# First value projection of a hybrid decoder on one core: tokens turned raw, the norm's root applied behind the matmuls, two column groups interleaved, the tiles normalized in place beside the last group

## The chip, the core and the metric

The kernel runs on one core of a Trainium2 chip. The core has a matrix engine (PE), a vector engine (DVE), an activation engine (ACT), GpSimd (POOL) and a queue engine (SP); DMAs are issued from SP, ACT and POOL. Each engine takes its instructions in a fixed order; what orders them between engines are semaphores. The metric is the device time of the program in microseconds (us), the median of its runs. Of a run one execution is profiled, and all rows below are of such an execution.

## What is computed

One step of a two-layer decoder: 1024 prompt tokens, 16 meta tokens and 8 x 8 sample tokens, 1104 rows of width 1024 in all. The change is in the first layer's input, of which these lines matter:

```python
def rmsnorm(x, g):
    r = lax.rsqrt(jnp.mean(xf * xf, axis=-1, keepdims=True) + EPS)
    return xf * r * g
...
p = xn @ w_in                       # xn = rmsnorm(h, norm_a): 1024 -> 3088 columns
q = heads(p[..., :HK]); k = heads(p[..., HK:2 * HK])
v = heads(p[..., 2 * HK:2 * HK + HV])      # 1024 columns of values
og = p[..., 2 * HK + HV:2 * HK + 2 * HV]
gi, gf = the last 16 columns        # gates: softcap, log_sigmoid of gf
```

Behind it come the mLSTM recurrence, a forgetting-attention layer that reads a paged cache (keys, values and per-row log-forget values, of which running sums are made), and two feed-forward layers. h itself is added again later, so the raw tokens are kept in DRAM too, turned (hD).

## The kernel before

All of the arithmetic is in fp32 by three matmuls a product: each operand is split in a high half (a rounding cast on ACT, "xh", "whi") and a low half (a subtraction on DVE, "xl", "wlo"), and PE multiplies high by high, high by low and low by high (`mm3`, L193 to L195). Tokens lie in nine tiles, the first of 80 (64 sample, 16 meta), the others of 128. The values need the tokens turned: features on the partitions, tokens along the row.

`load_x` (L628 on) does that tile by tile. A tile is loaded (xin, three buffers), squared and summed on ACT (L644), its root taken (L645, L646), and DVE multiplies it by root and gain (L647, the gain broadcast over the partitions in "gr"). PE turns the normalized tile in eight 128 x 128 transposes (xps, L655); they are split into xh and xl straight from the accumulator (L267, L268). PE also turns the raw tile (hps, L661), which ACT and DVE copy out (L662) and POOL writes to hD (L663).

Then four groups of value columns follow, c = 3, 0, 1, 2, of 256 columns each; c = 3 has the 16 gate columns beside it (272). Each tile of a group takes 24 matmuls into one of four accumulator banks (tmps), and ACT copies the bank out to the values vA (L695) and the gates (L697). Between them `row_mask` has POOL make masks (L2270 to L2273) that DVE reduces (L2275).

`cache_prep` loads 32 small pieces of the cache's log-forget values (lp, SP, L820), turns them (csps, L826), sums them along the row by a scan (L829), and writes the sums eight times to DRAM (csE, POOL, L832). In the listing it comes behind the values, and there its turn stands on PE.

Behind that, `wo_out` splits three blocks of the output weights, (load L252, cast L255, subtraction L256) and writes them to DRAM (woD, POOL, L717), and `qk_out` projects queries and keys: eight blocks of weights by three tile groups (336, 384 and 384 tokens; tiles 0-2, 3-5, 6-8), into two accumulator banks (mmA), taken out by ACT (stg, L732) and written by POOL (qkD, L733). Gate rows are turned between the first of these groups (rps, L903).

PE's order is written out by hand in `qk_out`; elsewhere a scheduler puts each engine's instructions in an order that respects buffers and data. Buffers come from pools: a tile of a tag waits until the tile that had its slot is done with. The weights of the values use three raw buffers and four for each half.

## Time and profile before

| | us |
|---|---|
| median of 3 runs (lowest, highest) | 2842.59 (2841.07, 2849.51) |
| the profiled execution | 2839.24 |
| its span, first to last instruction | 2837.5 |
| PE busy in the span | 2764.9 (97%) |
| DVE, ACT, POOL busy | 1772.9, 1166.4, 830.9 |

The granted clock of PE is 0.997 over the span. The time and the span differ by 1.7 us, which lie around the instructions. In a timeline row the columns are start and duration in us, engine, line, operation, output <- input, tile sizes and count; in brackets stands how long the engine was idle before and who ended that. A row of a group gives busy us in all and the mean ns of one instruction, then the idle time before.

### The profile page before, as it was taken

The numbers are of one execution on the slowest core, as the hardware profiler recorded it, in microseconds if no ns is written. First come the engines' busy times: TensorE is split into PE (matmuls) and PEld (weight loads), VectorE is DVE, ScalarE is ACT, GpSimd is POOL, SyncE is SP. The second block draws the span as 40 slices with busy tenths as digits, with TensorE's granted clock in tenths as the row PEclk, the third lists the DMA queues.
The fourth block names the chain that finished last, engine by engine and source line by source line (L and its number), as shares of the span: only waits on it lengthen the run. The fifth ranks groups of instructions, "written<-read, shape, count | busy, mean of one in ns | idle before, by whom it ended". The sixth has DMA issues, their size and how long they took to land. (4 is left out here: it accounts for less than half of the span.)

```text
span 2837.5 us, 60524 instructions
## 1 busy us (share of the span) xinstructions
PE 2764.9 (97%) x23614; PEld 2651.7 (93%) x23614; DVE 1772.9 (62%) x3921; ACT 1166.4 (41%) x2279; POOL 830.9 (29%) x1307
## 2 busy tenths in 40 slices
PE   7999998999999999999999999999999999999998
PEld 7999888999999999999999888677999999999998
DVE  5142566788888655573355443777478888765656
ACT  5232363333233233454344445877443323323345
POOL 3022233223223222224353202454312322323111
PEclk9999999999999999999999999999999999999999
DMA  6374537245555365644453686342524555526556
GB/s 193 113 207 136 146 107 273 81 130 168 176 168 160 111 211 187 201 155 153 145 173 136 218 302 231 129 168 88 156 76 135 168 176 169 161 90 231 183 193 214
DMA packets 428393, 469.45 MB, mean 165 GB/s; under 512 B 40030, under 2 KB 354522, under 8 KB 427082
## 3 DMA queue, kind: packets, MB, share of 16 engines
q1 hardware_dynamic: 378978, 316.78, 35.8%
q0 software_dynamic: 43600, 143.14, 15.2%
q10 hardware_dynamic: 5528, 5.65, 0.6%
q8 instruction: 186, 3.05, 0.4%
q14 instruction: 101, 0.83, 0.1%
HBM read 318.25 MB, written 147.21 MB: 164 GB/s over the span
## 5 line engine op out<-in xcount | busy, mean ns | idle before, releaser
L1416 PE MATMUL m<-xh,slot 128*128 128x276 f32 x2752 | 540.6, 290 | 1.8 <-ACT fs L1445 1.8
L1416 PEld LDWEIGHTS m<-xh,slot 128*128 128x128 f32 x2752 | 439.6, 188 | 3.7 <-ACT fs L1445 2.2
L1416 PE MATMUL m<-xl,slot 128*128 128x276 f32 x1376 | 397.1, 289 | 0.0
L1416 PEld LDWEIGHTS m<-xl,slot 128*128 128x128 f32 x1376 | 258.7, 188 | 0.0
L193 PE MATMUL tmps<-slot,xh 128*128 128x256 f32 (+2 forms) x864 | 243.1, 281 | 0.0
L195 PE MATMUL tmps<-slot,xl 128*128 128x256 f32 (+2 forms) x864 | 240.6, 278 | 0.0
L194 PE MATMUL tmps<-slot,xh 128*128 128x256 f32 (+2 forms) x864 | 240.5, 278 | 0.0
L268 DVE TENSOR_TENSOR slot<-slot,slot 128x1024 fp32r<-128x1024 f32 x124 | 162.7, 1313 | 59.4 <-ACT slot L267 57.9
L267 ACT CAST slot<-slot 128x1024 fp32r<-128x1024 f32 x124 | 129.5, 1045 | 141.4 <-PE m L1416 109.9
L194 PEld LDWEIGHTS tmps<-slot,xh 128*128 128x128 f32 (+1 forms) x864 | 159.2, 184 | 0.1
L195 PEld LDWEIGHTS tmps<-slot,xl 128*128 128x128 f32 (+1 forms) x864 | 158.6, 184 | 0.0
L193 PEld LDWEIGHTS tmps<-slot,xh 128*128 128x128 f32 (+1 forms) x864 | 158.4, 183 | 0.2
L193 PE MATMUL mmA<-xh,whi 128*128 128x384 f32 (+1 forms) x384 | 134.3, 350 | 0.1
L194 PE MATMUL mmA<-xl,whi 128*128 128x384 f32 (+1 forms) x384 | 127.4, 332 | 0.0
L195 PE MATMUL mmA<-xh,wlo 128*128 128x384 f32 (+1 forms) x384 | 127.2, 331 | 0.0
L268 DVE TENSOR_TENSOR slot<-vA,slot 128x1024 fp32r<-128x1024 f32 (+1 forms) x59 | 82.3, 1397 | 32.7 <-ACT slot L267 31.5
L268 DVE TENSOR_TENSOR slot<-Ht,slot 128x1024 fp32r<-128x1024 f32 (+1 forms) x59 | 82.0, 1393 | 32.8 <-ACT slot L267 31.6
L256 DVE TENSOR_TENSOR wlo<-wraw,whi 128x1024 fp32r<-128x1024 f32 (+1 forms) x32 | 39.0, 1225 | 101.0 <-ACT whi L255 78.0
L267 ACT CAST slot<-Ht 128x1024 fp32r<-128x1024 f32 (+1 forms) x59 | 60.9, 1037 | 95.5 <-PE m L1416 88.5
L267 ACT CAST slot<-vA 128x1024 fp32r<-128x1024 f32 (+1 forms) x59 | 60.8, 1035 | 95.4 <-PE m L1416 86.5
L1520 DVE TENSOR_TENSOR ws<-ws 128x128 f32<-128x128 f32 x264 | 93.8, 355 | 8.9
L2667 ACT ACTIVATE s<-s,nb 128x272 f32<-128x272 f32 (+7 forms) x126 | 98.9, 787 | 0.0
(788 smaller groups left out, 8666.2 us busy)
## 6 DMA issues: line engine op xcount, KB each, us to landing
ws<-in_w_down SPq DMA_DIRECT2D x176, 128.0 KB, 2.5
sD<-ws SPq DMA_DIRECT2D x176, 128.0 KB, 2.1
slot<-sD SPq DMA_DIRECT2D x40, 512.0 KB, 5.4
slot<-in_w_gate_up SPq DMA_DIRECT2D x36, 512.0 KB, 4.1
kp<-in_cache_k SPq DMA_DIRECT2D x32, 512.0 KB, 6.2
vp<-in_cache_v SPq DMA_DIRECT2D x32, 512.0 KB, 6.7
vA<-in_w_gate_up SPq DMA_DIRECT2D x26, 512.0 KB, 4.4
Ht<-in_w_gate_up SPq DMA_DIRECT2D x26, 512.0 KB, 3.9
```

What stands on the lines that cost most here:

```text
L193: mm(ps, sh, mh, start=first, stop=False)
L194: mm(ps, sh, ml, start=False, stop=False)
L195: mm(ps, sl, mh, start=False, stop=last)
L256: low = lambda: nc.vector.tensor_tensor(out=lo, in0=raw, in1=hi.bitcast(F32), op=ALU.subtract)
L267: self.nc.scalar.copy(hi, src)
L268: self.nc.vector.tensor_tensor(out=lo, in0=src, in1=hi.bitcast(F32), op=ALU.subtract)
L1416: nc.tensor.matmul(u.ps[h, b], w[p][:, k], x[q][:, k], start=first and k == i == 0, stop=k == 3 and i == 2, skip_group_check=True)
L1520: tt(out=o, in0=a, in1=b, op=ALU.subtract)
L2667: nc.scalar.activation(ss[z, u], ss[z, u], AF.Exp, bias=nb[:, z : z + 1], accum_out=sm[:, u, z : z + 1])
```

## The change

`values_a` takes the place of `load_x` and of the loop over groups.

- The raw tile is turned, once. The turned tile is split into xh and xl, and the same accumulator banks are copied to hD (two copies, both on DVE). The gain is put into the weights (`halve`: per 128 features a scaled cast on ACT and a fused multiply-subtract on DVE), and the root into the values, by ACT's scale as they leave the accumulator (`out`). Weights of a group come in two halves, raw buffers are two.
- Groups c = 3 and c = 0 are interleaved: c = 3 of tile i, the turn of tile i + 2, c = 0 of tile i - 2. Then c = 1, then c = 2.
- What follows needs xh and xl normalized. So each tile's raw copy is read back from hD (hr, three slots, POOL), scaled by the gain in eight ACT instructions and multiplied by the root on DVE (`scaled`; the roots go to DRAM as rD and come back broadcast, rb), and split again into the same xh and xl behind the tile's c = 2 matmuls.
- The cache sums move ahead of the fourth tile of c = 1, and their tiles (cp) use two of the three hr slots.
- Only the gain of this layer is loaded and turned at the start; the other 48 rows are loaded on POOL and turned during the interleaved groups. Row masks come last in the listing.

The diff's core:

```diff
-            rows = gp.tile([NG, P], F32, name="grows")
...
-                nc.scalar.dma_start(rows[at : at + n, :], src.rearrange("(k p) -> k p", p=P))
...
+            rows = gp.tile([8, P], F32, name="grows")
+            nc.scalar.dma_start(rows, I["norm_a"][0].rearrange("(k p) -> k p", p=P))
+            nc.scalar.activation(c.tile([P, 1], F32, name="root"), self.eps, AF.Sqrt)
+            ps = pp.tile([P, 8], F32, name="gps")
+            nc.tensor.transpose(ps, rows, self.ident[:8, :8])
+            nc.vector.tensor_copy(self.gain[:, G_A : G_A + 8], ps)
+
...
+    with ExitStack() as cw, self.pool("ppA0", bufs=4, space=PSUM) as pp:
+        self.wpools(cw, 2, 4)
+        xr = cw.enter_context(self.pool("xr", bufs=3, side="right"))
...
+        def fetch(c, z):
+            n = 272 if c == 3 else 256
+            c0 = 2 * HA * DK + 256 * c
+            raw = raws[c, z] = self.wp.tile([P, 4 * n], F32, name=self.uid("wraw"), tag="wraw", bufs=2).rearrange(
+                "p (k n) -> p k n", k=4)
+            get = lambda a, b: w_in[4 * z * P : 4 * z * P + 4 * P, a:b].rearrange("(k p) n -> p k n", p=P)
+            nc.sync.dma_start(raw[:, :, :256], get(c0, c0 + 256))
+            if c == 3:
+                nc.gpsimd.dma_start(raw[:, :, 256:], get(3072, 3088))
...
+        def halve(c, z):
+            raw = raws.pop((c, z))
+            n = raw.shape[2]
+            hi, lo = (self.wp.tile([P, 4 * n], F32R, name=self.uid(nm), tag=nm, bufs=4).rearrange(
+                "p (k n) -> p k n", k=4) for nm in ("whi", "wlo"))
+            for k in range(4):
+                nc.scalar.activation(hi[:, k], raw[:, k], AF.Copy, scale=G(4 * z + k))
+                nc.vector.scalar_tensor_tensor(out=lo[:, k], in0=raw[:, k], scalar=G(4 * z + k),
+                                               in1=hi[:, k].bitcast(F32), op0=ALU.mult, op1=ALU.subtract)
+            W[c, z] = hi, lo
+
+        def values(c, i):
+            n, m = 272 if c == 3 else 256, size(i)
+            ps = pp.tile([P, 512], F32, name=self.uid("tmps"), tag="mm0")
+            for k in range(KT):
+                h, l = self.x_tile(i, k)
+                wh, wl = W[c, k // 4]
+                self.mm3(ps[:m, :n], h, l, wh[:, k % 4], wl[:, k % 4], k == 0, k == KT - 1)
+
+            def out():
+                r = rr[:m, i : i + 1]
+                nc.scalar.activation(v(i)[:m, 2 * c : 2 * c + 2, :DV],
+                                     ps[:m, :256].rearrange("p (h d) -> p h d", h=2), AF.Copy, scale=r)
+                if c == 3:
+                    nc.scalar.activation(gates[:m, i, :], ps[:m, 256:272], AF.Copy, scale=r)
+            return out
+
+        with self.pool("lx") as lp, self.pool("lxp", bufs=4, space=PSUM) as tp:
+            junk = lp.tile([P, D], F32, name="xsq")
+
+            def load(i):
+                x = xin[i] = lp.tile([P, D], F32, name="xin", bufs=4)
+                if i == 0:
+                    nc.sync.dma_start(x[:NS], I["x_sample"].rearrange("b t d -> (b t) d"))
+                    nc.sync.dma_start(x[NS:T0], I["meta_tokens"])
+                else:
+                    nc.sync.dma_start(x, I["x_prompt"][0, (i - 1) * P : i * P, :])
+
+            def turn(i):
+                n = size(i)
+                for g in range(2):
+                    ps = xps[i, g] = tp.tile([P, 4, P], F32, name=self.uid("xps"), tag="xps")
+                    for k in range(4):
+                        f = 4 * g + k
+                        nc.tensor.transpose(ps[:, k, :n], xin[i][:n, f * P : (f + 1) * P], self.ident[:n, :n])
+
+            def halves(i):
+                n, (t0, t1) = size(i), TT[i]
+                for g in range(2):
+                    ks = slice(4 * g, 4 * g + 4)
+                    self.split(xps[i, g][:, :, :n], xh[:, ks, t0:t1], xl[:, ks, t0:t1])
+
+            def keep(i):
+                n, (t0, t1) = size(i), TT[i]
+                hs = lp.tile([P, KT, P], F32, name="hs", bufs=3)
+                for g in range(2):
+                    nc.vector.tensor_copy(hs[:, 4 * g : 4 * g + 4, :n], xps.pop((i, g))[:, :, :n])
+                nc.gpsimd.dma_start(self.hD[:, :, t0:t1], hs[:, :, :n])
+
+            def squares(i):
+                n = size(i)
+                nc.scalar.activation(junk[:n], xin.pop(i)[:n], AF.Square, accum_out=ss[:n, i : i + 1])
+                nc.scalar.activation(rr[:n, i : i + 1], ss[:n, i : i + 1], AF.Sqrt, scale=1.0 / D, bias=self.eps[:n])
+
...
+            with self.tc.manual_schedule(engines={E.DVE, E.Activation}):
+                for z in range(2):
+                    load(z)
+                    fetch(3, z)
+                load(2)
+                load(3)
+                turn(0)
+                halves(0)
+                halve(3, 0)
+                turn(1)
+                keep(0)
+                halve(3, 1)
+                squares(0)
+                halves(1)
+                keep(1)
+                for i in range(NT + 2):
+                    if i < NT:
+                        out = values(3, i)
+                    if i == 0:
+                        rows = xr.tile([P, P], F32, name="growsF", tag="rb")[: NG - G_F]
+                        self.gains(rows)
+                    if i + 2 < NT:
+                        turn(i + 2)
+                    if i == 0:
+                        squares(1)
+                    if i < NT:
+                        nc.vector.reciprocal(rr[: size(i), i : i + 1], rr[: size(i), i : i + 1])
+                        out()
+                    if i + 4 < NT:
+                        load(i + 4)
+                    if i + 2 < NT:
+                        halves(i + 2)
+                        keep(i + 2)
+                        squares(i + 2)
+                    if i < 2:
+                        fetch(0, i)
+                        halve(0, i)
+                    if i == 2:
+                        ps = tp.tile([P, 4, P], F32, name="gpsF", tag="xps").rearrange("p a b -> p (a b)")
+                        nc.tensor.transpose(ps[:, : NG - G_F], rows, self.ident[: NG - G_F, : NG - G_F])
+                        nc.vector.tensor_copy(self.gain[:, G_F:], ps[:, : NG - G_F])
+                    if NT - 1 <= i < NT + 1:
+                        fetch(1, i - NT + 1)
+                        halve(1, i - NT + 1)
+                    if i >= 2:
+                        values(0, i - 2)()
+            nc.gpsimd.dma_start(rD.rearrange("i p -> p i"), rr)
+
+        def scaled(i):
+            n, (t0, t1) = size(i), TT[i]
+            y = hr[i] = xr.tile([P, KT, P], F32, name=f"hr{i}", tag="hr")
+            rb = xr.tile([P, P], F32, name=f"rb{i}", tag="rb")
+            nc.gpsimd.dma_start(y[:, :, :n], self.hD[:, :, t0:t1])
+            nc.gpsimd.dma_start(rb, rD[i].partition_broadcast(P))
+            for k in range(KT):
+                nc.scalar.activation(y[:, k, :n], y[:, k, :n], AF.Copy, scale=G(k))
+            nc.vector.tensor_tensor(out=y[:, :, :n], in0=y[:, :, :n], in1=rb[:, :n].unsqueeze(1).broadcast_to([P, KT, n]),
+                                    op=ALU.mult)
...
+        with self.pool("cpp", space=PSUM) as cpp:
+            pages = self.cache_loads(xr)
+            for i in range(NT):
+                values(1, i)()
+                if i < 2:
+                    fetch(2, i)
+                    halve(2, i)
+                if i == 3:
+                    self.cache_prep(*pages, cpp)
+                if i > 5:
+                    scaled(i - 6)
+        for i in range(NT):
+            values(2, i)()
+            self.split(hr[i][:, :, : size(i)], xh[:, :, TT[i][0] : TT[i][1]], xl[:, :, TT[i][0] : TT[i][1]])
+            if i + 3 < NT:
+                scaled(i + 3)
+        for n, out in ((NQ, self.q8), (NM, self.m16)):
+            self.row_mask(kp.tile([P, P // n, n], F32, name=self.uid("rm"), tag="rm"), out, n)

...
-            self.load_x()
-            for c in (3, 0, 1, 2):
-                c0 = 2 * HA * DK + 256 * c
...
-                self.tm_proj([w_in[:, c0 : c0 + 256]] + ([w_in[:, 3072:3088]] if c == 3 else []), None, pp, "mm0", 4,
-                             evac)
-                if c == 3:
-                    for n, out in ((NQ, self.q8), (NM, self.m16)):
-                        self.row_mask(kp.tile([P, P // n, n], F32, name=self.uid("rm"), tag="rm"), out, n)
+        self.values_a(v, kp, gates, w_in)
...
-        self.cache_prep()
...
-def cache_prep(self):
+def cache_loads(self, xr):
...
+    a, b = (xr.tile([P, 2 * PAST], F32, name=f"cp{x}", tag="hr") for x in range(2))
...
+def cache_prep(self, lp, cs, lt, on, pp):
```

How this moves instructions is seen at three places. First **ACT**, from the eviction of the last value tiles (vA) on to the first outputs of the q/k projection (stg). Before, it has there:

```order
L695 COPY vA_100<-tmps_96_1533 128x2x128
L695 COPY vA_100<-tmps_97_1559 128x2x128
L695 COPY vA_100<-tmps_98_1585 128x2x128
L695 COPY vA_100<-tmps_99_1611 128x2x128
L827 ACTIVATE csl_1975<-csps_1977 128x512
L732 ACTIVATE stg_118_2181<-mmA_117_2156 128x336
L732 ACTIVATE stg_120_2209<-mmA_119_2184 128x384
```

and now the last cast of tiles 3 to 5 and all that ACT does for tiles 6 to 8 (hr6 to hr8) stand there:

```order
L271 CAST xh_92<-hr5_1674 128x8x128
L681 ACTIVATE vA_97<-tmps_77_1810,rr_126 128x2x128
L681 ACTIVATE vA_97<-tmps_78_1838,rr_126 128x2x128
L780 ACTIVATE hr6_1715<-hr6_1715,gain_69 128x128 x8
L780 ACTIVATE hr7_1756<-hr7_1756,gain_69 128x128 x8
L780 ACTIVATE hr8_1797<-hr8_1797,gain_69 128x128 x8
L271 CAST xh_92<-hr6_1715 128x8x128
L271 CAST xh_92<-hr7_1756 128x8x128
L681 ACTIVATE vA_97<-tmps_79_1866,rr_126 128x2x128
L271 CAST xh_92<-hr8_1797 128x8x128
L280 ACTIVATE lse_92_2197<-lse_92_2197 128x72
L852 ACTIVATE stg_100_2261<-mmA_99_2236 128x336
```

Between the evictions of two value tiles (tmps 78 and 79, the last two of c = 2) there are now 24 scalings and two casts; the cache's copy (csl) stands earlier.

Second **POOL**, whose DMAs here are the cache sums, the reloads of raw tiles (hr) and the broadcast roots (rb). Before:

```order
L717 DMA woD2_2014<-whi_108_2016 128x1024
L717 DMA woD2_2014<-wlo_109_2017 128x1024
L832 DMA csE_1645<-cs_1974 128x512 x8
L733 DMA qkD_101<-stg_118_2181 128x336
L733 DMA qkD_101<-stg_120_2209 128x384
```

Now:

```order
L837 DMA woD2_2094<-wlo_91_2097 128x1024
L777 DMA hr0_1472<-hD_88 128x8x80
L956 DMA csE_925<-cp0_927 128x512 x8
L777 DMA hr1_1511<-hD_88 128x8x128
L778 DMA rb3_1593<-rD_129 128x128
L777 DMA hr2_1550<-hD_88 128x8x128
L778 DMA rb4_1634<-rD_129 128x128
L778 DMA rb5_1675<-rD_129 128x128
L777 DMA hr3_1592<-hD_88 128x8x128
L777 DMA hr4_1633<-hD_88 128x8x128
L777 DMA hr5_1674<-hD_88 128x8x128
```

The reloads stand behind the eight writes of the sums, tiles 1 and 2 directly so, and each later tile waits for the split of the tile that had its slot (tile 3 for tile 0's).

Third **SP**, at the end of the cache pieces and the start of the next weights. Before:

```order
L820 DMA lp_1653<-in_cache_logf 128x16
L252 DMA wraw_101_1997<-in_w_out_a 128x8x128
L252 DMA wraw_104_2006<-in_w_out_a 128x8x128
L252 DMA wraw_107_2015<-in_w_out_a 128x8x128
L252 DMA wraw_114_2150<-in_w_in_a 128x8x128
L252 DMA wraw_126_2255<-in_w_in_a 128x8x128
L252 DMA wraw_138_2393<-in_w_in_a 128x8x128
```

Now:

```order
L940 DMA cp0_927<-in_cache_logf 128x16
L656 DMA wraw_57_1275<-in_w_in_a 128x4x256
L256 DMA wraw_83_2077<-in_w_out_a 128x8x128
L656 DMA wraw_61_1313<-in_w_in_a 128x4x256
L256 DMA wraw_86_2086<-in_w_out_a 128x8x128
L256 DMA wraw_89_2095<-in_w_out_a 128x8x128
L256 DMA wraw_96_2230<-in_w_in_a 128x8x128
```

The next weights (w_out, then w_in in blocks of 128 x 8 x 128) now have the two halves of c = 2's value weights (128 x 4 x 256) ahead and between, and those wait for a raw buffer, which c = 1's halves hold until they are scaled.

More of the change, by code (lines that the diff above doesn't have):

```diff
@@ L627, in load_x, with values_a @@
 @_add(Net)
[L628 removed]
+def values_a(self, v, kp, gates, w_in):
     nc, I = self.nc, self.I
[L631 to L663 removed]
@@ L812, in cache_prep @@
     self.pages = []
-    with self.pool("cp") as sp, self.pool("cpp", space=PSUM) as pp:
-        lp = sp.tile([P, NPG, NB, HB], F32, name="lp")
-        for b in range(NB):
-            for n in range(NPG):
-                j = b * NPG + n
-                v = nc.sync.value_load(self.ptab[0:1, j : j + 1], min_val=0, max_val=I["cache_k"].shape[0] - 1)
-                self.pages.append(v)
-                nc.sync.dma_start(lp[:, n, b, :], I["cache_logf"][bass.DynSlice(v, 1)].rearrange("a p h -> (a p) h"))
-        cs = sp.tile([P, PAST], F32, name="cs")
-        lt = sp.tile([P, PAST], F32, name="csl")
-        on = sp.tile([P, PAST], F32, name="cso")
-        ps = pp.tile([P, 512], F32, name="csps")
-        for n in range(NPG):
-            nc.tensor.transpose(ps[:, n * P : n * P + P], lp[:, n].rearrange("p b h -> p (b h)"), self.ident)
-        nc.scalar.activation(lt, ps, AF.Copy, scale=-1.0)
-        nc.gpsimd.memset(on, 1.0)
-        nc.vector.tensor_tensor_scan(cs, on, lt, 0.0, ALU.mult, ALU.add)
-        nc.vector.tensor_copy(self.clast, cs[:, PAST - 1 : PAST])
-        for q in range(NQ):
-            nc.gpsimd.dma_start(self.csE.rearrange("b (h q) k -> q b h k", q=NQ)[q].rearrange("b h k -> (b h) k"), cs)
@@ new lines, in cache_loads @@
+    return lp, a[:, PAST:], b[:, :PAST], b[:, PAST:]
+@_add(Net)
+def cache_prep(self, lp, cs, lt, on, pp):
+    nc = self.nc
+    ps = pp.tile([P, 512], F32, name="csps")
+    for n in range(NPG):
+        nc.tensor.transpose(ps[:, n * P : n * P + P], lp[:, n].rearrange("p b h -> p (b h)"), self.ident)
+    nc.scalar.activation(lt, ps, AF.Copy, scale=-1.0)
+    nc.gpsimd.memset(on, 1.0)
+    nc.vector.tensor_tensor_scan(cs, on, lt, 0.0, ALU.mult, ALU.add)
+    nc.vector.tensor_copy(self.clast, cs[:, PAST - 1 : PAST])
+    for q in range(NQ):
+        nc.gpsimd.dma_start(self.csE.rearrange("b (h q) k -> q b h k", q=NQ)[q].rearrange("b h k -> (b h) k"), cs)
```

72 lines of the change are left out of this document (24 added, 48 removed).

## The prediction

> **What bounds the kernel now.** I read the page's head first, then the busy time by stretches, then what PE waited for, and last the timelines at the places that the change touches.
>
> ```profile
> span 2837.5 us, 60524 instructions
> ...
> PE 2764.9 (97%) x23614; PEld 2651.7 (93%) x23614; DVE 1772.9 (62%) x3921; ACT 1166.4 (41%) x2279; POOL 830.9 (29%) x1307
> ```
>
> PE is the bound over the whole span, so an edit is worth what it takes from PE's work or idle time. By the order of the instructions everything behind the first projection stands as before; only the first 150 us can change. In stretches (columns: length, then busy us of PE, PEld, DVE, ACT, POOL, the granted clock, DMA share, GB/s):
>
> ```profile
> 0.00:20.00 20.00, 7.90 (x42) 6.71 (x42) 6.64 (x14) 9.36 (x16) 17.68 (x117) 1.00 0.72 206
> 20.00:60.00 40.00, 34.63 (x278) 32.79 (x277) 27.16 (x40) 25.11 (x58) 7.63 (x12) 1.00 0.73 234
> 60.00:105.00 45.00, 42.02 (x363) 41.59 (x362) 12.53 (x12) 16.60 (x31) 3.21 (x6) 1.00 0.60 180
> 105.00:143.00 38.00, 38.00 (x338) 38.00 (x338) 0.00 (x0) 5.15 (x15) 0.00 (x0) 1.00 0.01 2
> ```
>
> PE is idle for 12.1, 5.4 and 3.0 us in the first three stretches, 20.5 us in all; then it is full, at 38.00 / 338 = 0.1125 us a matmul of 256 columns, with nearly no DMA. What it waited for up to 143 us:
>
> ```profile
> PE hps L661 <- ACT hs L662: 5.8, 3, 2.4
> PE gps L222 <- POOL rm L2273: 5.7, 1, 5.7
> PE hps L661 <- DMA xin<-in_x_prompt: 5.1, 3, 4.1
> PE tmps L193 <- ACT vA L695: 3.0, 2, 1.7
> ```
>
> So at most 20.5 us of idle time and the work that is dropped can be won. The milestones on PE:
>
> ```profile
> 5.91 1.33 PE L661 MATMUL hps<-ident,xin 80*128 80x80 f32 x8
> 11.32 1.09 PE L661 MATMUL hps<-ident,xin 128*128 128x128 f32 x4 [4.09 <-DMA xin<-in_x_prompt]
> 17.72 0.57 PE L193 MATMUL tmps<-whi,xh 128*80 128x272 f32 x1
> 22.91 0.60 PE L661 MATMUL hps<-ident,xin 128*128 128x128 f32 x4
> 52.66 1.06 PE L655 MATMUL xps<-ident,xn 128*128 128x128 f32 x8
> 65.53 0.29 PE L195 MATMUL tmps<-whi,xl 128*128 128x272 f32 x1
> 65.66 0.28 PE L193 MATMUL tmps<-whi,xh 128*80 128x256 f32 x1
> 142.67 0.60 PE L826 MATMUL csps<-ident,lp 128*128 128x128 f32 x4
> 146.84 0.34 PE L193 MATMUL mmA<-xh,whi 128*128 128x384 f32 x1
> ```
>
> The first value matmul comes at 17.72, the first group (c = 3) ends at 65.66, the fourth at 142.67, and the second tile group of the q/k projection, "x1" below, starts at **146.84**. It is the mark I use, since what follows it is ordered alike in both kernels.
>
> **Part 1: the head.** 72 transposes go (one turn of a tile instead of two); at 1.06 us for eight that is 9.5 us of PE at the most. The normalizing multiplies of DVE (L647) and the load of the broadcast gain go too. Tile 0 can be turned at 5.9 as before, tile 1 at about 11.3, since its load still stands behind others on SP; and with c = 3 and c = 0 interleaved each tile gives PE 24 matmuls of 272 columns (0.13 apart, 65.53 to 65.66; a shade less on average, 0.126) and 24 of 256: 3.0 + 2.7 + 0.85 for a turn = 6.6 us. A tile moves 1 MB (512 KB in, 512 KB of transposed copy out), about 4.5 us at 234 GB/s, so the transfers keep ahead after the first two tiles. Work left at 11.3: 27.2 + 24.3 + 8 x 0.85 = 58.3. For stalls I take 3.3 us: the two first weight halves have to land, and a DVE reduction of the row masks now stands among the first weight splits and waits for POOL, which has seven more DMA issues ahead of those masks. Bounds: 0, and 6.3, by which the head would start no sooner than before. c = 0 ends at **73**, c = 3 three tiles of c = 0 earlier, at 65. Before, two groups were through at 65.66 + 24.3 = 90, so 17 us are in hand here.
>
> **Part 2: the third group** needs 24.3 us of PE and the four transposes of csps, and ends at 98. If the fourth followed at PE's pace it would end at 122, and x1 would come some 20 us sooner than now. It can't, for what the change puts there.
>
> **Part 3: when the last group's normalization can start.** The raw tiles come back from DRAM into three slots; two of these hold the cache sums until csE is written. csE waits for the scan, the scan for ACT's copy of csps, and that copy stands behind the fifth cast of the next weights on ACT.
>
> ```profile
> 80.40 1.05 ACT L255 CAST whi<-wraw 128x1024 fp32r<-128x1024 f32 x1 [6.00 <-DMA wraw<-in_w_out_a]
> 97.65 1.04 ACT L255 CAST whi<-wraw 128x1024 fp32r<-128x1024 f32 x1 [3.38 <-DMA wraw<-in_w_in_a]
> ```
>
> ```profile
> 76.01 7.09 SPq L252 DMA_DIRECT2D wraw<-in_w_out_a  x3
> 84.27 11.38 SPq L252 DMA_DIRECT2D wraw<-in_w_in_a  x3
> ```
>
> From the first issue at 76.01 to the fifth cast at 97.65 pass 21.6 us. In the changed kernel the first of these issues stands behind a value-weight load that needs a raw slot, free once ACT has scaled the first half of c = 1, and that needs c = 3 to be done: 65 plus about 4 (four scalings, an eviction, a table load) = 69. One value-weight load more stands among them, so half a turn of 4.7 us (the spacing of those casts) is added: cast at 93.
>
> ```profile
> 144.00 1.23 DVE L829 TENSOR_TENSOR_SCAN cs<-cso,csl 128x512 f32<-128x512 f32 x1 [40.00 <-ACT csl L827]
> ```
>
> ```profile
> 145.68 4.26 POOL L832 DMA_DIRECT2D csE<-cs  x8 [55.00 <-DVE lf_tm L891]
> ```
>
> ```profile
> L832 POOL DMA_DIRECT2D csE<-cs x8: 539/539/547, 145.7 to 149.4; - x8
> ...
> DMA to landing us min/median/max: 2.3/3.3/4.0
> ```
>
> Cast 1.05, copy 0.6, and 1.7 from scan to first csE issue: 96.4. The eight writes took up to 149.4 + 4.0 - 145.7 = 7.7 us when the queues were otherwise quiet. Now they share with weight loads and with the woD writes, for which I take 11.5; bounds 7.7 and twice that, 15.4. All landed: 108.
>
> **Part 4: three batches of three tiles.** Each raw tile is reloaded, scaled by the gain in eight ACT instructions, multiplied by the root on DVE, cast on ACT and subtracted on DVE. The nearest rows:
>
> ```profile
> L663 POOL DMA_DIRECT2D hD<-hs x9: 844/853/1022, 14.8 to 46.3; - x9
> ...
> DMA to landing us min/median/max: 4.2/5.3/7.2
> ```
>
> ```profile
> L261 ACT ACTIVATE slot<-slot,gain 128x128 fp32r<-128x128 f32 x56 | 19.3, 401 | 8.3 <-PE bps L194 4.3 <-PE bps L195 3.2
> ```
>
> ```profile
> L267 ACT CAST xh<-xps 128x512 fp32r<-128x512 f32 x16 | 8.8, 593 | 2.1 <-PE xps L655 1.8
> L695 ACT COPY vA<-tmps 128x256 f32<-128x256 f32 x32 | 11.8, 372 | 46.7 <-PE tmps L195 46.7
> ```
>
> ```profile
> L256 DVE TENSOR_TENSOR wlo<-wraw,whi 128x1024 fp32r<-128x1024 f32 x14 | 16.9, 1222 | 40.1 <-ACT whi L255 36.6 <-DMA woD<-wlo 3.5
> ```
>
> Eight scalings are 8 x 19.3 / 56 = 2.76 us a tile; the cast is 1.05 (the L255 rows), the subtraction 1.22. The multiply with a broadcast operand is not in the trace; between 0.7 (half of it) and 1.3 it is off the chain in any case, beside ACT's next scaling. The read of hD isn't either; its write of the same size is nearest, 5.3, with 4.2 and 7.2 as ends. The third tile's slot is free at 108: 0.3 + 5.3 + 2.76 + 0.37 (eviction) + 0.7 (cast of the 80-token tile) + 0.85 gives the first subtraction's end at 118. Only then may tile 3 be reloaded, and ACT's order holds its cast until tiles 4 and 5 are scaled: 0.3 + 5.3 + 8.3 + 0.4 + 1.05 + 1.2 = **16.5 us a batch**, where PE's work on three tiles is 8.1. Second batch: 134.6. The third: 0.3 + 5.3 + 8.3 + 2.1 (casts 6 and 7), then the eviction of the last value tile, 0.4, which stands behind all of these on ACT: 151.0. x1 needs that bank, so **x1 starts at 151.0 against 146.84: +4.2 us**. The log-sigmoid and the root copy of the gates have 5 us and more before PE asks for them, and hide as they do now.
>
> On the profiled execution (2839.24 us, 3.4 under the median) that is 2843.4; on the median of 2842.59 it is **2846.8**, given as 2847. A measurement here tells about 0.3%, 8.5 us, from no change.
>
> **The clock.** After PE's longest wait four transposes took 1.09 us against 0.60 at 22.91, and the granted clock of that stretch is 1.00. PE will wait 6 us or more just before x1. The Trainium skill ("TensorE: Matmul & The Clock Gate", Part 1, "What's actually happening") has the array at half rate after an idle window of about 3.4 us until it has been busy as long; by that I estimate 1.7 us more behind this wait, and the clock of 1.00 over the 4.09 us wait does not bear it out.
>
> **The rivals.**
> - **Faster: the reloads hide.** If slots came free soon enough, ACT alone would bound the last group: 9 x (2.76 + 1.05 + 0.37) = 37.6 us from 97 to 134.6, 12 us sooner than now: 2830. For it: ACT has 5 us of work in 105 to 143 now. Against it: three slots, and each reload ordered behind a subtraction. Chance 0.12.
> - **Slower: the reloads and csE are crowded.** At 7.2 us for each of three reloads (+5.7) and 15.4 for csE (+3.9) x1 comes 13.8 later than now: 2856. It decides from 1.4 us a reload above my 5.3 on. For it: software-queue transfers beside the weight loads took up to 7.2; against it: 105 to 143 was quiet. Chance 0.22.
> - **Slower: the head doesn't start early,** held by DVE behind POOL's masks. If the first value matmul stays at 17.7, all of the chain behind c = 3 is 6.3 - 3.3 = 3 us later than I have it, and stalls on the way add as much again: 2853. It decides if c = 3 ends after 69.3. Chance 0.15.
> - **The clock falls back** after the wait before x1: x1's 24 matmuls, 4.2 us at 0.1735 each, take twice as long: 2851. Chance 0.05.
>
> **How the numbers follow.** The forecast has 0.46. Within 0.3% (2834.1 to 2851.1) lie the forecast and the clock: 0.51. Slower by more are the crowded reloads and the late head: 0.37. Faster by more: 0.12. All low bounds at once (csE 7.7, reloads 4.2, no stalls) give 4.2 - 3.8 - 3.3 - 3.3 = -6.2, all high ones +4.2 + 3.9 + 5.7 + 3 = +16.8. The range runs from the ACT-bound case to a little past the crowded one: 2830 to 2857.
>
> **What would show it.** In the profile after: the first value matmul near 11 to 12; c = 0 and c = 3 through by 73; the first csE issue near 96 and its last landing near 108; PE waiting several us two or three times behind ACT's evictions in the last group; ACT's eight-fold scalings in three bursts some 16 us apart; x1 near 151 behind ACT. I am wrong if PE runs the last group without waits (then 2830 or less), if the head gains nothing, or if the times behind x1 don't shift with it.

## The result, and the profile after

The changed kernel takes **2870.41 us** (median of 4 runs, 2869.61 to 2872.75), the kernel before 2843.16 beside it (4 runs). The ratio is 1.0095, 95% interval 1.008 to 1.011: 27 us slower, where 2847 was forecast and 2857 was the end of the range. The profiled execution took 2872.75. Its page head:

```profile
span 2871.0 us, 60567 instructions
...
PE 2778.9 (97%) x23543; PEld 2668.1 (93%) x23543; DVE 1790.9 (62%) x3965; ACT 1198.6 (42%) x2375; POOL 847.4 (30%) x1333
```

PE has 71 matmuls fewer and is busy 14 us longer: some of its work runs slower. The first stretches, with the columns of the prediction's table (the granted clock is the third number from the end):

```profile
0.00:20.00 20.00, 10.04 (x63) 9.16 (x64) 8.72 (x22) 9.48 (x20) 19.35 (x115) 1.00 0.74 222
20.00:60.00 40.00, 37.39 (x311) 37.12 (x310) 21.47 (x47) 26.06 (x62) 9.40 (x21) 1.00 0.62 188
60.00:105.00 45.00, 39.94 (x322) 39.53 (x321) 12.07 (x22) 16.49 (x34) 7.00 (x12) 0.96 0.61 173
105.00:143.00 38.00, 24.12 (x181) 23.31 (x180) 11.38 (x12) 19.50 (x54) 10.96 (x17) 0.87 0.63 179
143.00:200.00 57.00, 50.68 (x304) 49.13 (x305) 35.48 (x61) 31.22 (x67) 12.86 (x21) 0.91 0.41 123
```

In the first 60 us PE does 374 matmuls instead of 320: the head gains. From 105 to 143, where it was full with 338, it does 181 and is idle for 14 us, at a lower clock. What it waited for up to 200 us:

```profile
PE tmps L193 <- ACT vA L681: 19.3, 6, 6.2
PE mmA L193 <- ACT vA L681: 5.4, 1, 5.4
PE xps L704 <- DMA xin<-in_x_prompt: 4.0, 1, 4.0
PE gpsF L764 <- issue: 2.6, 1, 2.6
```

25 us are waits for accumulator banks that ACT had not yet emptied. PE's timeline at the marks of the prediction:

```profile
12.09 0.57 PE L193 MATMUL tmps<-whi,xh 128*80 128x272 f32 x1
67.56 0.29 PE L195 MATMUL tmps<-whi,xl 128*128 128x272 f32 x1
143.35 0.58 PE L193 MATMUL tmps<-whi,xh 128*128 128x256 f32 x1 [6.21 <-ACT vA L681]
162.62 0.69 PE L193 MATMUL mmA<-xh,whi 128*128 128x384 f32 x1 [5.36 <-ACT vA L681]
163.11 0.52 PE L194 MATMUL mmA<-xl,whi 128*128 128x384 f32 x1
163.43 0.52 PE L195 MATMUL mmA<-xh,wlo 128*128 128x384 f32 x1
167.24 0.33 PE L195 MATMUL mmA<-xh,wlo 128*128 128x384 f32 x1
167.41 0.34 PE L193 MATMUL mmA<-xh,whi 128*128 128x384 f32 x1
168.98 0.78 PE L1027 MATMUL rps<-ident,gates 80*8 80x80 f32 x6
```

The first value matmul and the end of c = 3 are near the forecast; x1 is at 162.62, not 151.0. Behind the 5.36 us wait the matmuls stand 0.32 apart until about 167 and then 0.17: half speed for some 4 us. In before the gate rows (rps) were at

```profile
151.02 0.78 PE L903 MATMUL rps<-ident,gates 80*8 80x80 f32 x6
```

so there the loss is 18.0 us. SP's queue at the place that the prediction's Part 3 starts from:

```profile
42.96 38.95 SPq L940 DMA_DIRECT2D cp<-in_cache_logf  x32
82.02 0.39 SPq L656 DMA_DIRECT2D wraw<-in_w_in_a  x1
82.46 0.50 SPq L256 DMA_DIRECT2D wraw<-in_w_out_a  x1
83.05 0.53 SPq L656 DMA_DIRECT2D wraw<-in_w_in_a  x1
```

The first w_out load is at 82.46, forecast 69. Ahead of it stand the 32 loads of cache pieces, 1.22 us each. Each of them now has a read of its page number from memory into SP's registers right ahead of it. This is the view of one line's instructions on SP, of after (start of the first and of the last at the end):

```profile
L938 SPq TENSOR_LOAD <-ptab x32: 263/269/917, 41.7 to 80.8; - x32
L938 SPq FUSED_REGOPS  x32: 152/152/181, 42.5 to 81.2; - x32
```

and the same line of before, where the reads began at 29.3 and 28 of them were over when the loads started at 55.5:

```profile
L818 SPq TENSOR_LOAD <-ptab x32: 262/270/1595, 29.3 to 74.9; - x32
```

SP's loads of before show both paces in one queue. The first 26 took 0.54 us each; of the last six, four have their read right ahead and start 1.12 us apart (from 71.17 on):

```profile
55.50 14.12 SPq L820 DMA_DIRECT2D lp<-in_cache_logf  x26
70.64 5.33 SPq L820 DMA_DIRECT2D lp<-in_cache_logf  x6
```

ACT behind it (fifth cast, then scalings in bursts):

```profile
108.33 1.04 ACT L259 CAST whi<-wraw 128x1024 fp32r<-128x1024 f32 x1 [4.95 <-DMA wraw<-in_w_in_a]
...
124.85 2.44 ACT L780 ACTIVATE hr<-hr,gain 128x128 f32<-128x128 f32 x8 [10.43 <-DMA hr<-hD]
...
138.05 4.89 ACT L780 ACTIVATE hr<-hr,gain 128x128 f32<-128x128 f32 x16 [3.99 <-DMA hr<-hD]
...
153.19 7.13 ACT L780 ACTIVATE hr<-hr,gain 128x128 f32<-128x128 f32 x24 [1.91 <-DMA hr<-hD]
160.23 1.97 ACT L271 CAST xh<-hr 128x1024 fp32r<-128x1024 f32 x2
162.11 0.46 ACT L681 ACTIVATE vA<-tmps,rr 128x256 f32<-128x256 f32 x1
```

and POOL (the roots written to DRAM and read back, csE written, tile 2 reloaded behind it, then tiles 3 and 6):

```profile
60.13 1.06 POOL L771 DMA_DIRECT2D rD<-rr  x1
72.79 1.67 POOL L778 DMA_DIRECT2D rb<-rD  x3 [11.61 <-DMA rD<-rr]
...
112.07 4.28 POOL L956 DMA_DIRECT2D csE<-cp  x8 [11.30 <-DVE clast L954]
...
123.56 0.90 POOL L777 DMA_DIRECT2D hr<-hD  x1 [4.34 <-DMA csE<-cp]
...
133.34 0.90 POOL L777 DMA_DIRECT2D hr<-hD  x1 [0.42 <-issue]
...
148.67 0.90 POOL L777 DMA_DIRECT2D hr<-hD  x1 [0.95 <-DVE xl L272]
```

The chain is the one forecast: cast, sums, csE, then reloads that each wait for a subtraction, 133.34 to 148.67 = 15.3 us a batch, and the last eviction behind 24 scalings and two casts.

### The profile page after: what moved, and what is told of

Same layout as the page of the kernel before. It is cut to its first block, busy times and chain, and to the rows that moved or that the text cites. A ratio compares the mean times of both kernels' runs of the same rounds, so it can differ in the third digit from the quotient of the medians.

```text
span 2871.0 us, 60567 instructions
## 1 busy us (share of the span) xinstructions
PE 2778.9 (97%) x23543; PEld 2668.1 (93%) x23543; DVE 1790.9 (62%) x3965; ACT 1198.6 (42%) x2375; POOL 847.4 (30%) x1333
## 4 chain that ended last, share of the span: by engine, by line
PE 78%; DVE 6%; issue 5%; DMA 4%; ACT 3%; SPq 1%; POOL 1%; DVEq 0%; POOLq 0%; ACTq 0%
PE m L1540 30%; PE dps L1879 16%; PE tmps L193 3%; PE tmps L195 3%; PE tmps L194 3%; PE pops L195 2%; PE pops L193 2%; PE pops L194 2%; PE sp L2764 2%; PE op L2851 1%; PE mmA L193 1%; DVE s L2768 1%; PE mmA L194 1%; PE mmA L195 1%; PE tp L2818 1%
## 5 line engine op out<-in xcount | busy, mean ns | idle before, releaser
L193 PE MATMUL tmps<-whi,xh 128*128 128x256 f32 (+3 forms) x288 | 85.5, 297 | 19.3 <-ACT vA L681 19.3
L272 DVE TENSOR_TENSOR slot<-vA,slot 128x1024 fp32r<-128x1024 f32 (+1 forms) x59 | 81.9, 1391 | 33.2 <-ACT slot L271 32.2
L272 DVE TENSOR_TENSOR slot<-Ht,slot 128x1024 fp32r<-128x1024 f32 (+1 forms) x59 | 81.9, 1390 | 32.7 <-ACT slot L271 31.5
```

Of the source, the lines that this page charges most:

```text
L193: mm(ps, sh, mh, start=first, stop=False)
L272: self.nc.vector.tensor_tensor(out=lo, in0=src, in1=hi.bitcast(F32), op=ALU.subtract)
```

## The experiments

The theory after this reading: the last group's chain sets x1 as forecast; it starts late because of the reads on SP (P); the clock halves behind the wait (C); and PE's pace is lower because the new one-column tile "root" moves every tile behind it, xh and xl among them, by 32 bytes (S). The rival to P is that the batches of reloads set x1 whatever comes before them (B); the rival to S is that a change in the traffic slows the matmuls. Times are medians of the runs; before measured 2843.1 to 2843.7 beside them.

**Placement (S).** e2_no_shift is after with the root's dummy result in a spare column, so that no tile moves; e3_before_shifted is before with a one-column tile more.

```diff
-            nc.scalar.activation(c.tile([P, 1], F32, name="root"), self.eps, AF.Sqrt)
+            nc.scalar.activation(rm[:, NQ + NM : NQ + NM + 1], self.eps, AF.Sqrt)
```

```diff
+        nc.vector.memset(c.tile([P, 1], F32, name="pad"), 0.0)
```

> The changed kernel, but the one-column output of the early root instruction goes to a spare column of the row-mask tile, so that no 32 bytes are added to the constants and all tiles behind them lie where they lay before. Theory S (the 32 bytes move xh, xl and the weight slots, and 256-column matmuls then start 0.117 us apart instead of 0.113): the spacing is 0.113 to 0.114 again in the value groups and in the later key/value projection, the head ends 2 to 3 us sooner and the total is 8 to 11 us less, 2860 to 2863. Rival D (the slower pace is that of one chip or run, or of the clock): spacing 0.117 and total 2868 to 2872.

> The kernel before, with one column of padding (32 bytes) behind the row masks in the constants and nothing else. Theory S: 256-column matmuls of the value groups 0.117 us apart instead of 0.113, total 2850 to 2854. Rival D: 2841 to 2845, spacing 0.113.

e2: 2861.36 (2857.93 to 2861.83), ratio to before 1.0062 (1.0046 to 1.0079): 9.0 under after. x1 comes 2.4 earlier:

```profile
160.23 0.69 PE L193 MATMUL mmA<-xh,whi 128*128 128x384 f32 x1 [5.49 <-ACT vA L681]
```

e3: 2854.67 (2852.63 to 2856.58), ratio 1.0042 (1.0028 to 1.0056): 11 us slower with nothing changed but where tiles lie and one small memset. So the placement costs time, whichever of the two kernels it is changed in. Not all that was expected of e2 came: the first tile of c = 1 runs at 0.113 us a matmul instead of 0.117 in after, but the head ended later, not sooner (c = 3 through at 70.5 instead of 67.9). In that execution the 28 matmuls from 29.15 to 35.1 ran at half rate, 0.213 apart, behind the wait for the second turn of gains; in after's they didn't. A difference of a microsecond or two between single executions has to be read with this in mind. To find which places are good, before was also moved by 64 bytes (e5_before_pad64, a pad of 16 columns), by 96 (e12_before_pad96, 24 columns) and by 32 downwards (e11_before_back32, no instruction added):

```diff
-        self.clast = c.tile([P, 1], F32, name="clast")
         rm = c.tile([P, P], F32, name="rowm")
+        self.clast = rm[:, NQ + NM : NQ + NM + 1]
```

> The kernel before with 64 bytes of padding in the constants where the earlier run had 32. Theory S64 (what counts is where a tile starts modulo 64 bytes): spacing of the 256-column matmuls 0.113 us again and a total of 2841 to 2846. Rival (any move of the tiles costs, or it is the padding instruction): 0.117 and 2850 to 2857 as with 32 bytes.

> The kernel before with its one-column tile clast put into a spare column of the row masks, so that every tile behind it lies 32 bytes lower instead of higher. Theory any-move (the placement of before happens to be the good one): slower than before by 5 to 11 us, value matmuls of 256 columns .117 to .119 us apart instead of .113. Theory block (what counts is where the split tiles lie within a block of 128 bytes; before they lie 32 into one, 64 and 96 into it were slower): the start of a block has not been tried; if the lower half of a block is the good one, 2841 to 2845 and .113 apart; if only 32 into it is, 2849 to 2855.

> The kernel before with 96 bytes more ahead of the split tiles, by which they lie at the start of the next block of 128 bytes. Theory block: the same pace and, within 3 us, the same time as the run with the tiles 32 bytes lower, which lies at the start of a block too. Theory any-move: 2848 to 2855 whatever that run gives, with the pace of this run unrelated to that one's.

The same stretch of 35 us, in which PE is full at clock 1.00, in before:

```profile
105.00:140.00 35.00, 35.00 (x311) 35.00 (x311) 0.00 (x0) 4.64 (x13) 0.00 (x0) 1.00 0.01 3
```

and in e11:

```profile
105.00:140.00 35.00, 35.00 (x296) 35.00 (x295) 0.00 (x0) 4.48 (x12) 0.00 (x0) 1.00 0.03 10
```

| tiles moved by | median (lowest to highest) | ratio (95%) | matmuls in 105 to 140 us |
|---|---|---|---|
| 0 (before) | 2843.1 to 2843.7 | | 311 |
| -32 | 2855.18 (2852.86 to 2857.13) | 1.0041 (1.0027 to 1.0055) | 296 |
| +32 | 2854.67 (2852.63 to 2856.58) | 1.0042 (1.0028 to 1.0056) | 300 |
| +64 | 2850.41 (2847.62 to 2855.6) | 1.0028 (1.0019 to 1.0038) | 298 |
| +96 | 2860.85 (2859.58 to 2861.3) | 1.0061 (1.0044 to 1.0077) | 295 |

All four moves cost 7 to 18 us, and the value matmuls run at 0.117 to 0.119 us instead of 0.1125. With e11 the added memset is out as a cause, and with the quiet stretch (next to no DMA) traffic is too. The guess of e5, that +64 is as good as 0, fell; so did that of e11 and e12, that two places 128 bytes apart are alike (2855.18 and 2860.85), and e12 is above the 2848 to 2855 of any-move too. The pace in the stretch doesn't rank the times either. That before's place is the best of the five is shown; which relation of addresses makes it so stays open. Nor does the place alone set the pace: in e2, tiles 1 and 2 of c = 2 run at 0.113 and tiles 3 to 8, with the same weights but behind a wait, at 0.118, while in e10 below tiles 1 to 8 all run at 0.113. No run here separates what switches it.

**The late cache pieces (P).** In e1_pages_early the 32 reads stand among the token loads:

```diff
                     if i + 4 < NT:
                         load(i + 4)
+                        for j in range(8 * i - 8, 8 * i) if i else ():
+                            self.pages.append(nc.sync.value_load(...))
...
-            v = nc.sync.value_load(...)
+            v = self.pages[j]
```

> The changed kernel, but SP reads the 32 page numbers into registers between the early token loads, where it waits anyway, instead of one right ahead of each cache-piece load. Theory P (the pieces' pace on SP, 38.95 us for 32 where the kernel before took about 19.5, holds the next weights' loads and with them csE, the reloads and x1): the pieces take 18 to 20 us, the first w_out load is issued near 74 instead of 82.5 (then the raw slot of the value weights holds it), x1 starts near 154 instead of 162.6, total 2861 to 2863. Rival B (the three batches of reloads set the end whatever comes before them): the pieces are early and x1 stays within 2 us of 162.6, total 2869 to 2872. Rival Q (the early register reads hold the head's loads): the first w_out load earlier, but c = 0 ends 3 us or more after 76, total 2865 to 2872.

The 32 loads then took 19.75 us, and x1 came at 155.87, 6.8 earlier. c = 0 ended at 76.4 as in after, so the early reads don't hold the head (Q). But the time was 2869.02 (2868.5 to 2869.96), ratio 1.009 (1.0073 to 1.0107). The scheduler of SP now put the three w_out loads (from 65.69) ahead of c = 2's value weights (82.94), and ACT's order changed with it: rps waited 3.4 us for ACT's copy of a gate row, which stood behind the scaling of tile 8. Two things had changed, so between P and B it decided nothing. e9_pages_only keeps the reads early and writes SP's order out by hand over the w_out loads too:

```diff
-        cw.enter_context(self.tc.manual_schedule(engines={E.PE, E.SP}))
+        cw.enter_context(self.tc.manual_schedule(engines={E.PE}))
...
+        sp.enter_context(self.tc.manual_schedule(engines={mybir.EngineType.SP}))
         self.values_a(v, kp, gates, w_in)
```

> The changed kernel (tiles shifted as there) with the register reads moved as in the earlier run, and now SP's order written out over the first w_out loads too, so that these stay behind the value weights and the orders of ACT, DVE and POOL stay those of the changed kernel. Theory P: the pieces take 18 to 20 us, the first w_out load is issued between 73 and 76 instead of 82.5, csE, the reloads and x1 move by the same 7 to 9 us (x1 at 154 to 156), total 2861 to 2864. Rival B (the group's own batches set x1 whatever comes before): x1 within 2 us of 162.6, total 2868 to 2872.

It took 2861.9 (2861.05 to 2866.27), ratio 1.0061 (1.0045 to 1.0076), 8.5 under after; the profiled execution, at 2866.27, is 6.5 under after's. SP's queue:

```profile
45.42 19.59 SPq L945 DMA_DIRECT2D cp<-in_cache_logf  x32
72.28 3.98 SPq L656 DMA_DIRECT2D wraw<-in_w_in_a  x2
76.32 10.70 SPq L256 DMA_DIRECT2D wraw<-in_w_out_a  x3
```

0.61 us a load instead of 1.22; w_out starts 6.1 earlier and x1, at 156.61, 6.0 earlier. The time is as P had it, w_out (76.32) and x1 just miss P's bounds, and B falls: x1 did move. Both runs with the reads early bring x1 forward by 6 to 7 us, so that the late pieces cost about this much of x1 is shown. How the gain travels is less clean, since ACT's order did not quite stay after's: the copy of csps now comes ahead of the fifth cast (102.27) and not behind it.

```profile
99.43 0.59 ACT L956 ACTIVATE cp<-csps 128x512 f32<-128x512 f32 x1
```

By this csE is first issued at 101.86, 10.2 earlier than in after, and 4.2 of these are lost again on the way to x1. No run moves the reads alone.

**The batches of the last group.** e4_left_raw leaves out the reload, the scaling and the second split, so the q/k projection and all behind it work on raw tokens. Two further kernels, both on top of e2, keep the work: e7_scale_on_dve does gain and root in one DVE instruction per 128 features and takes the eight scalings off ACT, and e8_five_slots gives four of the nine tiles the raw weight buffers as further slots.

```diff
             for k in range(KT):
-                nc.scalar.activation(y[:, k, :n], y[:, k, :n], AF.Copy, scale=G(k))
-            nc.vector.tensor_tensor(out=y[:, :, :n], ...)
+                nc.vector.scalar_tensor_tensor(out=y[:, k, :n], in0=y[:, k, :n], scalar=G(k), in1=rb[:, :n],
+                                               op0=ALU.mult, op1=ALU.mult)
```

```diff
+            if i in (1, 2, 6, 7):
+                y = self.wp.tile([P, KT * P], F32, name=f"hr{i}", tag="wraw", bufs=2).rearrange(...)
...
-                if i > 5:
-                    scaled(i - 6)
+                if i > 3:
+                    scaled(i - 4)
...
-            if i + 3 < NT:
-                scaled(i + 3)
+            if i + 5 < NT:
+                scaled(i + 5)
```

> The changed kernel without the reload, scaling, multiplication and second split of the tiles: what follows the values reads the raw tiles (left out: the normalization of what the q, k and gate projections read). It shows what the reloads cost in all. Theory P + B: PE runs the third and fourth group with the waits on the weights' casts alone, x1 starts between 130 and 137, total 2838 to 2846. Rival: if the clock's half rate behind the waits, or the late weights, cost most of it, x1 starts after 140 and the total is above 2848.

> The changed kernel with the tiles unshifted (2861.4 us, x1 at 160.2), and the eight ACT scalings and the DVE multiplication of a reloaded tile replaced by eight DVE instructions that multiply by gain and root at once. Theory B (a batch's period is load + 3 x ACT's scalings + cast + subtraction = 15.4 us): the casts no longer wait behind scalings, the period falls to 10 us or less, x1 starts between 146 and 151, total 2848 to 2853. Rival (the reloads' landing or the clock holds the group, ACT is not what counts): x1 after 155 and total above 2856.

> The changed kernel with the tiles unshifted (2861.4 us, x1 at 160.2), where tiles 1, 2, 6 and 7 are reloaded into the two raw weight buffers, free by then, and all reloads are called two tiles sooner: five slots instead of three, and the first reloads no longer behind csE. Theory B: ACT's 37 us of scalings, casts and evictions then run nearly without waits; x1 starts between 148 and 153, total 2849 to 2855. Rival (csE and the late weights hold tile 0, and with it all, whatever the slots): x1 within 3 us of 160, total 2858 to 2862.

e4: 2851.91 (2848.66 to 2855.52), ratio 1.0027 (1.0016 to 1.0037); 18.5 under after, with x1 at 144.78. That is the rival's case (x1 after 140, above 2848) and not the expected one. Its waits:

```profile
PE tmps L193 <- ACT vA L681: 8.7, 3, 3.9
```

Even without any reload, evictions stand behind the casts of weights that arrive late, and pace and cache pieces are as in after. rps comes at 149.02, 2.0 ahead of before, so the 8 us that are left lie behind it. e7: 2854.42 (2853.26 to 2858.4), ratio 1.004 (1.0026 to 1.0054), 6.9 under e2; x1 at

```profile
155.03 0.69 PE L193 MATMUL mmA<-xh,whi 128*128 128x384 f32 x1 [4.37 <-ACT vA L681]
```

e8: 2853.1 (2848.8 to 2856.4), ratio 1.0027 (1.0016 to 1.0039), 8.3 under e2, with rps at 159.79 where e2 had 166.65. x1 of e8 is at 155.55. Both miss their expected x1 (151 and 153 at the latest), and e7 its time by 1.4 us. csE starts at 110.14 and 108.94, as late as in e2 (108.82). In e7 tiles 1 and 2 still wait for it (reloaded at 115.45 and 121.49), and a batch takes 11.9 us (129.71 to 141.59) where e2's took 15.7 and 10 at most was expected. In e8 tiles 1 and 2 are back early (reloaded at 88.06 and 91.68); tiles 3 and 4 now take the two slots of the cache sums and come back at 115.31 and 121.02. So the scalings on ACT and the number of slots each cost about 7 to 8 us, and the late start hides part of what each would give.

**The clock (C).** e6_kept_busy does the first tile group of the projection twice, into the same bank, so that PE works where it waited for x1's bank (a single execution):

```diff
-                    self.fm_cols(ps[:, :n], wh, wl, self.XG[t])
+                    for _ in range(2 if m == t == 0 else 1):
+                        self.fm_cols(ps[:, :n], wh, wl, self.XG[t])
```

> The changed kernel with the first group of the q/k projection done twice into the same bank (24 matmuls of 336 columns, 3.7 us more of PE work, put into the 5.4 us wait ahead of x1). Theory C (PE's clock halves after a wait of some 5 us): the wait ahead of x1 falls to 1.5 to 2 us, x1 still starts within 1 us of 162.6, and its 384-column matmuls come 0.174 us apart from the first instead of 0.32; what follows x1 comes 2 us sooner. Rival (0.32 is the cost of the first matmuls of x1 whatever came before, for instance of its weights' landing): the spacing stays 0.32.

The waits of e6 have 1.3 us where after had 5.4:

```profile
PE tmps L193 <- ACT vA L681: 17.7, 5, 5.5
...
PE mmA L193 <- ACT vA L681: 1.3, 1, 1.3
```

Behind it the matmuls of x1 are 0.176 apart from the third on, not 0.32. x1 started 1.9 later than in after in this execution, at 164.49, and the third group began at 170.13 against 170.27: 2.0 us of x1's time had been the clock. So the spacing came out as theory C has it, and the start of x1 and what follows it did not (within 1 us and 2 us sooner were expected): rps and the third group are only 0.1 earlier. In this execution the first w_out load had already come 1.0 later than in after's, at 83.48. The time was 2871.49; one execution can't tell it from after's.

**All of it at once.** e10_all_four is e9 with the placement of e2, the DVE scaling of e7 and the slots of e8.

> Tiles unshifted, register reads early with SP's order as in the run beside it, five slots, and gain and root in one DVE pass. If the three costs of the last group (late pieces, three slots, scalings on ACT) are separate, the gains of 7, 8 and 8 us add up against 2861.4: 2838 to 2841, x1 near 138 to 140. If they are one wait counted three times (each removes what the others would), no more than the largest: 2850 to 2854. I expect between: x1 between 138 and 146, total 2839 to 2847, about as fast as the kernel before.

It took 2841.4 (11 runs, 2839.89 to 2849.62) against 2843.21 (15 runs) of before: ratio 0.9994 (0.9985 to 1.0003). The 27 us are gone; a gain can't be told from none. x1 is at 142.33, within what was expected, as is the time. Its marks on PE and what is left of the waits:

```profile
146.60 0.78 PE L1035 MATMUL rps<-ident,gates 80*8 80x80 f32 x6
```

```profile
PE tmps L193 <- ACT vA L681: 9.8, 3, 6.8
PE xps L704 <- DMA xin<-in_x_prompt: 4.4, 1, 4.4
PE gpsF L769 <- issue: 2.6, 1, 2.6
```

rps comes 4.4 us earlier than in before; the medians differ by 1.8. The 9.8 us are evictions behind the weight casts, whose loads are now the late ones:

```profile
109.73 1.04 ACT L259 CAST whi<-wraw 128x1024 fp32r<-128x1024 f32 x1 [8.35 <-DMA wraw<-in_w_in_a]
```

The four parts measured one by one sum to 9.0 + 8.5 + 6.9 + 8.3 = 32.7 us; together they gave 2870.41 - 2841.4 = 29.0. They overlap little. The orders moved along here too: ACT's copy of csps comes behind the third cast, and csE starts at 96.21 instead of 112.07, so e10 shows that these four edits together remove the loss, and not how much of it each removes there.

## Why the prediction was wrong

The kind of loss was right, and its size wrong by a factor of more than six: 4.2 us were forecast and 27.3 measured.

| step | forecast | measured |
|---|---|---|
| first value matmul | 11 to 12 | 12.09 |
| end of c = 3 | 65 | 67.56 + 0.29 |
| end of c = 0 | 73 | 76.14 |
| first w_out load | 69 | 82.46 |
| from it to the fifth cast | 24 | 25.9 |
| csE, first issue to all landed | 11.5 | 11.4 |
| one batch of three tiles | 16.5 | 15.3 |
| from the first w_out load to x1 | 82.0 | 80.2 |
| x1 | 151.0 | 162.62 |

- **The head (Part 1)** was right within 3 us. Its start is as worked out (11.3 and 0.85 for the turn of tile 1, measured 12.09). By c = 3's end at 67.9 it is 2.9 us behind the forecast. The 216 matmuls of 272 columns took 1.4 more than 0.126 each, half of it in the first six, which stand up to 0.37 and mostly 0.23 apart behind the 4.0 us wait for tile 1. The 144 of 256 columns up to there took 1.2 more than 0.1125 each, and the two waits (1.0 for xl, 2.6 for the second turn of gains) are 0.3 above what was taken for stalls.
- **The step that failed is in Part 3: "65 plus about 4 (four scalings, an eviction, a table load) = 69".** It asked only when the raw slot comes free. SP's queue was not walked: 32 loads stand ahead of these, each with its register read, and they hold it from 42.96 to 81.9. The piece of SP's order that was shown begins with the last of these loads. e9 shows what this was worth: 6.0 us of x1, and 6.5 to 8.5 of the time. The other 7.3 us of the 13.5 remain in e9. Its first value-weight load comes at 72.28, when ACT has scaled the first half of c = 1 (70.03 to 71.74), 3.3 later than the 69 of the forecast. Its second stands ahead of w_out there and waits for the scaling of the other half (73.63 to 75.33); it comes at 75.87, and w_out at 76.32.
- **Part 4, and the rest of Part 3,** were right within 2 us over a chain of 82. Borrowed rows (the write of hD for the read, other ACT scalings for these) did well: the reloads took 5.6 us to land at the median, where 5.3 was taken. The raised guess for csE is what was measured. Neither the crowded reloads nor the late head decided.
- **The clock was set aside too easily.** The granted clock is 0.87 from 105 to 143, and x1's matmuls show the half rate row by row. Four transposes at 1.09 us against 0.60 in before were a sign of it, and the 1.00 of a long stretch was taken as stronger. That 1.00 measured nothing: the trace of before holds no record of the clock ahead of 19.5 us, that of after none ahead of 13.6, and the view gives 1.00 there. The Trainium skill ("TensorE: Matmul & The Clock Gate", Part 1, "What's actually happening") is borne out behind the 5.36 us wait: half rate, and full rate again after some 4 us; my 1.7 us estimated from it measured 2.0. In after's view of two stretches, the first has 1.00 for matmuls 0.227 apart that stand 0.126 apart later; the second, behind x1's wait, has a record and gives the half:

```profile
12.00:13.50 1.50, 1.50 (x9) 1.50 (x8) 1.22 (x4) 1.49 (x4) 1.50 (x12) 1.00 0.61 240
160.50:167.00 6.50, 4.38 (x14) 4.38 (x15) 6.15 (x11) 3.61 (x6) 0.00 (x0) 0.50 0.01 3
```

- **The pace was no term at all.** "Everything behind the first projection stands as before" was read off the order of instructions; it says nothing on where their tiles lie. e2 puts 9.0 us to it. Most of this lies behind rps, where the prediction had no change: in e3, the kernel before with its tiles moved alike, rps comes 2.8 later and the time is 11.0 longer.

As a sum, with the parts up to rps from the profiled executions: 18.0 us are lost there (4.2 forecast, 13.5 from the later start, less 1.8 on the chain, plus 2.0 for the clock), and the other 9.3 of the 27.3 come behind it, near the 8.2 that the placement alone costs there in e3. This split is good to a few us only, since it sets single executions against medians: the profiled one of after took 2.3 more than its median, that of before 3.9 less.

## What to carry to other kernels

Where a step hangs on a transfer, walk the issuing queue from the last known row to it and price every instruction there, register reads too: a load whose address is read just ahead of it cost twice a plain one. A loss in a chain of buffers is found by moving one start at a time; afterwards compare the engines' orders, since an edit that moves a load can move a copy past a cast. What each part gives alone, beside all of them together, shows whether the parts overlap. And a change that adds even one column to a pool of constants is two changes; move it to a spare column before timing the idea.

## What was not expected of the hardware

- Moving the tiles by 32, 64 or 96 bytes made the same matmuls of 256 columns 4 to 5% slower (311 in 35 us before, 295 to 300 moved, all at clock 1.00), and the whole kernel 7 to 18 us. In e2 two paces, 0.113 and 0.118, occur with the same weights in the same place.
- A register read and the register operation behind it take 0.27 + 0.15 us and more around them, on SP's queue: 1.22 us a load with one ahead in after against 0.61 without in e9, and 1.12 against 0.54 within before.
- The column of roots, written to DRAM in pieces of 4 bytes (rD), was issued at 60.13, and the first read of it could only start at 72.79, with POOL idle for 11.6 us until it had landed (first rows of POOL above). Here that cost nothing, as the first reload came at 99.86.
